# A two-block transformer step on one core: the weight-tile splits near a norm, taken from GpSimd and given to VectorE

## The chip, the core and the metric

The kernel runs on one core of one Trainium2 chip. The metric is device time in microseconds (us) of one execution; lower is better. A core has engines that run side by side, each with its own queue of instructions that it works through in order: TensorE (PE in the profile, its weight loads PEld), VectorE (DVE), ScalarE (ACT), GpSimd (POOL), and SyncE (SP), which here only issues the DMA transfers that bring tiles from device memory.

## The reference

256 tokens of width 1024 go through two blocks, all in float32:

```
first_block:  h = rmsnorm(x); z = h @ w_in
              pool branch, dilated attention, gates;  x = x + merged @ w_out; x = rmsnorm(x) * final_gain
second_block: x += short_conv(rmsnorm(x))
              x += peer(rmsnorm(x))         # 256 tokens against 16384 experts
              x += windowed_gqa(rmsnorm(x))
              x += peer(rmsnorm(x))
              return rmsnorm(x)
peer(xn):     q = xn @ w_q; two top-16 lists of 128 sub-keys per head and token, best 16 pairs g, idx
              out = sum over the 16 of  g * gelu(xn . u[idx]) * v[idx]
```

`peer` is done as two dense products over all 16384 rows of `u` and of `v`, with the chosen weights scattered between them.

## The kernel before

**Splits.** Products are made at float32 accuracy from three matmuls on a faster 32-bit type (`fp32r`): an operand is cut into `hi`, its rounding to that type, and `lo = operand - hi`. Then `a @ b` is `ah@bh + ah@bl + al@bh` (lines 136 to 138). Each weight tile of 128x1024 arrives by DMA as `raw` (four buffers, so that a transfer waits until an older tile has been split), is rounded by ScalarE (`hi`, line 122) and subtracted by `split_now` (`lo`, line 123). Line 123 is given to VectorE or to GpSimd: to GpSimd on every `pool_share`-th tile where a caller asks for that, and also for the first `RELIEF` = 3 streamed tiles behind each norm (`last_rows` sets the counter `relief`).

**Norms.** Between two stages x is updated, normed and transposed. `last_rows` writes this order out by hand: the last products of a stage for token half 1, meanwhile the norm of half 0, then the norm of half 1. The norm of a half is a chain. VectorE adds the two accumulator halves to x (line 234), multiplies by the gain (`xn`, line 303), sums up the mean square (`m`, line 246; into the conv stage `n`, lines 377 and 379), and makes the inverse root in nine tiny steps, lines 256 to 263. It then scales `xn` (line 319, the other half on ScalarE, line 320). TensorE transposes `xn` (line 391), ScalarE and VectorE split the result (`xh`, `xl`, lines 328 and 329), and only then can the next stage multiply. While this goes on for half 1, TensorE has only `first(0)`: the products of half 0 with the first 512 columns of the next stage's weights, held in four tiles `enh`/`enl` that `Enter.split` makes (lines 297 and 298). Of these four, the third (`c == 2`) has its `enl` made by GpSimd, and the other three by VectorE.

**What sets the order.** Outside the hand-written stretches, a list scheduler orders each engine's instructions by priorities. Splits are made ahead of their place (`AHEAD`), norm steps have the highest priority (`CHAIN`), and the result is one fixed queue for each engine. An engine never passes over an instruction that waits.

**The stages**, in us of the profile: first block to 294, conv mixer to 397, first peer to 1208, attention to 1310, second peer to 2115. In the conv mixer the last of eight tiles `o7` is made by VectorE from `pr` (lines 746, 750, 752, 756) and split (lines 402, 403) before the stage's last products; in the first block the last two tiles `mt6`, `mt7` play that part (lines 561, 563, 402, 403).

**Peer queries.** A peer stage begins with sixteen query tiles; n = 4 to 15 go through `dense_t` with `pool_share` 2, so that every second one has its `lo` made by GpSimd.

Of the kernel before, what the change touches and what calls it, by code (L numbers as in the profile page):

```python
# [32 lines left out]
AHEAD, KEEP, CHAIN = 200, 100, 4000  # L33
HL = 3
WARM = 14
RELIEF = 3


JOBS, TURN, J1, J2, LATE, XA = 35, 4, 40, 124, 6, 100
# [11 lines left out]
def two_blocks(ctx: ExitStack, tc: tile.TileContext, io, out):  # L51
    nc = tc.nc
    V, S, G, PE, SY = nc.vector, nc.scalar, nc.gpsimd, nc.tensor, nc.sync
# [18 lines left out]
    def bank(which, name):  # L72
        return which.tile([P, 512], F32, tag="b", name=name)
# [14 lines left out]
           allow_small_or_imprecise_dtypes=True)  # L88


    count, relief, fetched, pin, pinned = [0], [0], [0], [None], [0]
    last_split = [None]

    more = []
# [1 line left out]
    def fetch(src):  # L96

        fetched[0] += 1
        if more and fetched[0] % 3 == 1:
            raw = more[-1].tile([P, D], F32, tag="more", name="more")  # L100
        else:
            raw = stream.tile([P, D], F32, tag="raw", name="raw", bufs=4)
        SY.dma_start(out=raw, in_=src)
        return raw

    def split(raw, pool_share=0, into=None):
        with tc.high_priority(offset=AHEAD):
            return split_now(raw, pool_share, into)

    def split_now(raw, pool_share, into):  # L110
        count[0] += 1
        hi, lo = into or [stream.tile([P, D], F32R, tag=t, name=t, bufs=HL) for t in ("hi", "lo")]
        on_pool = pool_share and count[0] % pool_share == 0
        if relief[0] > 0 and into is None:
            relief[0] -= 1
            on_pool = True
        if pinned[0] > 0 and into is None:
            pinned[0] -= 1
            with tc.issue_after(pin[0]):
                S.copy(out=hi, in_=raw)  # L120
        else:
            S.copy(out=hi, in_=raw)  # L122
        low = (G if on_pool else V).tensor_tensor(out=lo, in0=raw, in1=hi.bitcast(F32),  # L123
                                                  op=OP.subtract)
        if not on_pool:
            last_split[0] = low.ins
        return hi, lo
# [5 lines left out]
    def products(ps, pairs, first, last):  # L133
        n = len(pairs)
        for i, ((ah, al), (bh, bl)) in enumerate(pairs):
            PE.matmul(out=ps, lhsT=ah, rhs=bh, start=first and i == 0, stop=False)  # L136
            PE.matmul(out=ps, lhsT=ah, rhs=bl, start=False, stop=False)  # L137
            PE.matmul(out=ps, lhsT=al, rhs=bh, start=False, stop=last and i == n - 1)  # L138

    def dense_t(src, acts, pool_share=0):  # L140

        ah, al = acts
        hi, lo = split(fetch(src), pool_share)
        ps = bank(p_mm, "mm")[:, :T]
        products(ps, [((hi[:, k * P:(k + 1) * P], lo[:, k * P:(k + 1) * P]), (ah[:, k], al[:, k]))
                      for k in range(8)], True, True)
        return ps
# [48 lines left out]
    def last_rows(nxt, acc0, acc1, steps, scale=None):  # L196


        n = len(steps)
        with tc.manual_schedule(engines={EN.PE, EN.DVE, EN.Activation}):  # L200
            if acc0:
                for half in range(2):
                    add_half(0, half, acc0[half], scale)
                for half in range(2):
                    nxt.added(0, half)
                r = nxt.inverse(0)
                nxt.scaled(0, r)
            for j, step in enumerate(steps):
                if acc0 and j == nxt.turn_at:
                    nxt.turn(0)  # L210
                step()
                if j == n // 2 - 1:
                    add_half(1, 0, acc1[0], scale)
                if j == max(n // 2 - 1, acc0 and nxt.turn_at or 0):
                    nxt.added(1, 0)
            add_half(1, 1, acc1[1], scale)
            nxt.added(1, 1)
            r = nxt.inverse(1)
            nxt.scaled(1, r)
            nxt.first(0)  # L220
            nxt.turn(1)
            nxt.first(1)
            for a in range(2):
                nxt.after(a)
        relief[0] = RELIEF

    def add_half(a, half, acc, scale=None):
        with tc.high_priority(offset=CHAIN):
            s = slice(half * 512, (half + 1) * 512)
            if scale:  # L230
                V.scalar_tensor_tensor(out=x[:, a, s], in0=acc, scalar=scale, in1=x[:, a, s],  # L231
                                       op0=OP.mult, op1=OP.add)
            else:
                V.tensor_tensor(out=x[:, a, s], in0=acc, in1=x[:, a, s], op=OP.add)
            sum_squares(a, half)
# [38 lines left out]
    class Enter:  # L274
# [16 lines left out]
        def split(self, c, d0=0, d1=D, engine=None):  # L291
            if d0 == 0:
                self.kept.append([self.new([P, D], F32R, f"en{w}{c}") for w in "hl"])
            hi, lo = [t[:, d0:d1] for t in self.kept[c]]
            with tc.high_priority(offset=KEEP):
                raw = self.raw[c] if self.raw else fetch(self.columns[c])
                S.copy(out=hi, in_=raw[:, d0:d1])  # L297
                (engine or (G if c == 2 else V)).tensor_tensor(  # L298
                    out=lo, in0=raw[:, d0:d1], in1=hi.bitcast(F32), op=OP.subtract)

        def added(self, a, half, engine=None):
# [462 lines left out]
    def gqa_mixer(entered, nxt):  # L764
        acts, nat = (xh, xl), entered.nat
        with ExitStack() as es:
# [111 lines left out]
            for step in range(18):  # L878
# [42 lines left out]
                if step >= 14:  # L921
                    nxt.split(step - 14)
                    for half in range(2):
                        row(acc1[half], step - 14, 1, half)
            last_rows(nxt, None, acc1, [lambda half=half, n=n: row(acc1[half], n, 1, half)
                                        for half in range(2) for n in range(4, 8)])

    def peer(l, entered, nxt):
        acts, nat = (xh, xl), entered.nat
        with ExitStack() as es:  # L930
            with ExitStack() as es1:
# [19 lines left out]
                def query(n):  # L951
                    if n < 4:
                        q[n] = first[:, n]
                        return
                    ps = dense_t(io["peer_w_q"][l, n - 4], acts, 2)
                    q[n] = X[1][:, n].rearrange("p g t -> p (g t)")
                    S.copy(out=q[n], in_=ps)

# [23 lines left out]
                for n in range(5):  # L982
                    query(n)
# [176 lines left out]
                for i in range(P):  # L1160
# [3 lines left out]
                    for job in at.get(i, []):  # L1164
# [6 lines left out]
                    ps = dense_t(io["peer_u"][l, i], acts, int(i < len(by_pool) and by_pool[i])).rearrange(  # L1171
                        "p (g t) -> p g t", t=4)
# [39 lines left out]
            for i in range(P):  # L1212
# [9 lines left out]
                for a in range(2 if i < P - LATE else 1):  # L1222
                    row(i, a, (0, 1), act, wt)
            last_rows(nxt, acc[0], acc[1], [lambda half=half, n=n, w=w: row(P - LATE + n, 1, [half], *w)
                                            for half in range(2) for n, w in enumerate(late)],
                      1 / G_SCALE)
# [153 lines left out]
```

## Time and profile before

| | |
|---|---|
| median of 3 runs | 2125.38 us (2123.36 to 2125.76) |
| the profiled execution | 2124.93 us, of which 2123.2 us are the span of the profile |
| TensorE busy | 2088.4 us (98%) |
| VectorE busy | 1507.1 us (71%) |
| ScalarE busy | 1092.9 us (51%) |
| GpSimd busy | 218.0 us (10%), 119 instructions |
| DMA | 373.94 MB, mean 176 GB/s |

Busy is the share of the span in which an engine had an instruction under way, and an instruction that has started but is held up counts as busy too. A row of the timeline gives the start, the duration, the engine, the line, the operation, out<-in and the shape; xN means that N alike in a row were put together, and the bracket gives the idle time of the engine before it and what ended it.

### The profile page before, as it was taken

What the parts mean: (1) busy time and instruction counts of PE and PEld (TensorE: products, weight loads), DVE (VectorE), ACT (ScalarE), POOL (GpSimd) and SP (SyncE); (2) the same over time, 40 slices, a digit from 0 to 9 for tenths busy, and PEclk for the clock granted to TensorE, in tenths of its full rate; (3) what the DMA queues carried; (4) which work ended last, traced back from release to release, by engine and by line L of the source; (5) the groups of instructions that cost most, each with busy time, mean ns of one, the idle gap of its engine ahead of it and who ended that gap; (6) DMA issues with size and microseconds to landing.
All of it is one profiled execution on the core that took longest, in us unless ns stands there. A gap on an engine that the chain in (4) does not pass through costs nothing. (4 is left out here: it accounts for less than half of the span.)

```text
span 2123.2 us, 37690 instructions
## 1 busy us (share of the span) xinstructions
PE 2088.4 (98%) x14288; PEld 1897.6 (89%) x14288; DVE 1507.1 (71%) x3101; ACT 1092.9 (51%) x1971; POOL 218.0 (10%) x119
## 2 busy tenths in 40 slices
PE   8999999999999999999999999999999999999998
PEld 7899989899999999888888877999999998888886
DVE  4456778699778887665667485998778885565565
ACT  4556645345555444555556474455554445555553
POOL 3220010263000000000000142540000000000000
PEclk9999999999999999999999999999999999999999
DMA  6645737256655555666667461566555556666663
GB/s 232 221 129 159 236 121 237 91 170 179 183 165 159 161 164 165 191 194 189 192 194 264 146 225 37 173 181 187 160 160 161 167 160 198 191 193 191 190 206 120
DMA packets 104437, 373.94 MB, mean 176 GB/s; under 512 B 12096, under 2 KB 14144, under 8 KB 103744
## 3 DMA queue, kind: packets, MB, share of 16 engines
q1 hardware_dynamic: 103968, 371.01, 56.3%
q8 instruction: 112, 1.84, 0.3%
q14 instruction: 69, 0.57, 0.1%
q10 hardware_dynamic: 288, 0.52, 0.1%
HBM read 370.44 MB, written 1.05 MB: 175 GB/s over the span
## 5 line engine op out<-in xcount | busy, mean ns | idle before, releaser
L136 PE MATMUL mm<-xh,hi 128*128 128x256 f32 x2880 | 830.2, 288 | 0.4 <-DVE k_l L636 0.4
L123 DVE TENSOR_TENSOR lo<-raw,hi 128x1024 fp32r<-128x1024 f32 x532 | 651.9, 1225 | 248.9 <-ACT hi L122 245.6
L137 PE MATMUL mm<-xl,hi 128*128 128x256 f32 x2880 | 813.8, 283 | 0.0
L138 PE MATMUL mm<-xh,lo 128*128 128x256 f32 x2880 | 813.7, 283 | 0.0
L122 ACT CAST hi<-raw 128x1024 fp32r<-128x1024 f32 x600 | 630.0, 1050 | 338.8 <-PE mm L137 188.4
L136 PEld LDWEIGHTS mm<-xh,hi 128*128 128x128 f32 x2880 | 550.8, 191 | 2.6 <-issue 1.3
L137 PEld LDWEIGHTS mm<-xl,hi 128*128 128x128 f32 x2880 | 551.2, 191 | 0.3
L138 PEld LDWEIGHTS mm<-xh,lo 128*128 128x128 f32 x2880 | 550.7, 191 | 0.0
L1204 PE MATMUL acc<-hi,al 128*128 128x512 f32 x976 | 304.4, 393 | 0.5 <-DVE al L1194 0.5
L1204 PE MATMUL acc<-lo,ah 128*128 128x512 f32 x976 | 302.4, 391 | 0.0
L1204 PE MATMUL acc<-hi,ah 128*128 128x512 f32 x976 | 301.8, 390 | 0.2 <-ACT ah L1193 0.2
L1204 PEld LDWEIGHTS acc<-hi,ah 128*128 128x128 f32 x976 | 182.9, 188 | 42.6 <-ACT ah L1193 1.0
L1204 PEld LDWEIGHTS acc<-hi,al 128*128 128x128 f32 x976 | 183.1, 188 | 41.2 <-DVE al L1194 1.8
L1204 PEld LDWEIGHTS acc<-lo,ah 128*128 128x128 f32 x976 | 183.3, 188 | 38.8
L1193 ACT CAST ah<-xa 128x256 fp32r<-128x256 f32 x200 | 81.2, 407 | 241.5 <-PE acc L1204 241.5
L123 POOL TENSOR_TENSOR lo<-raw,hi 128x1024 fp32r<-128x1024 f32 x70 | 173.0, 2473 | 305.8 <-ACT hi L122 291.4
L1194 DVE TENSOR_TENSOR al<-xa,ah 128x256 fp32r<-128x256 f32 x200 | 85.0, 426 | 99.0 <-PE acc L1204 99.0
L1109 DVE TENSOR_TENSOR o<-iota_k,ij 128x1024 f16<-128x1024 f16 x128 | 88.2, 689 | 48.5 <-PE G L1123 48.2
L1133 ACT COPY xa<-G 128x240 f32<-128x240 f32 (+22 forms) x92 | 24.1, 262 | 148.2 <-DVE xa L1130 148.2
L1116 DVE TENSOR_TENSOR wi<-o,gt 128x512 f16<-128x512 f16 x256 | 96.5, 418 | 1.2
L298 POOL TENSOR_TENSOR enl<-raw,enh 128x1024 fp32r<-128x1024 f32 x5 | 12.6, 2524 | 813.8 <-ACT enh L297 813.8
L1123 PE MATMUL G<-wi,o 128*128 128x128 f16 x1024 | 79.8, 220 | 0.0
(461 smaller groups left out, 2016.4 us busy)
## 6 DMA issues: line engine op xcount, KB each, us to landing
raw<-in_peer_u_dram SPq DMA_DIRECT2D x256, 512.0 KB, 3.6
raw<-in_peer_v_dram SPq DMA_DIRECT2D x256, 512.0 KB, 3.6
raw<-in_peer_w_q_dram SPq DMA_DIRECT2D x24, 512.0 KB, 3.8
raw<-in_conv_w_in_dram SPq DMA_DIRECT2D x20, 512.0 KB, 4.5
raw<-in_w_rest_dram SPq DMA_DIRECT2D x18, 512.0 KB, 3.7
raw<-in_w_qk_dram SPq DMA_DIRECT2D x16, 512.0 KB, 4.5
more<-in_w_rest_dram SPq DMA_DIRECT2D x10, 512.0 KB, 3.6
raw<-in_w_v_dram SPq DMA_DIRECT2D x8, 512.0 KB, 4.0
```

Of the source, the lines that this page charges most:

```text
L122: S.copy(out=hi, in_=raw)
L123: low = (G if on_pool else V).tensor_tensor(out=lo, in0=raw, in1=hi.bitcast(F32), op=OP.subtract)
L136: PE.matmul(out=ps, lhsT=ah, rhs=bh, start=first and i == 0, stop=False)
L137: PE.matmul(out=ps, lhsT=ah, rhs=bl, start=False, stop=False)
L138: PE.matmul(out=ps, lhsT=al, rhs=bh, start=False, stop=last and i == n - 1)
L1109: V.tensor_tensor(out=o.rearrange("p n (b c) -> p n b c", c=4), in0=iota_k.rearrange("p (b c) -> p b c", c=4).unsqueeze(1).to_broadcast(fo ...
L1116: V.tensor_tensor(out=wi[i].rearrange("p n (b c) -> p n b c", c=4), in0=o[:, 0:4].rearrange("p n (b c) -> p n b c", c=4), in1=gt[i][:, s]. ...
L1123: PE.matmul(out=ps[:, :, t], lhsT=o[:, 4 + t], rhs=wi[i][:, t], start=i == 0, stop=i == 1)
L1133: S.copy(out=dst[:, old:], in_=ps[:, i0 + old:i0 + n])
L1193: S.copy(out=act[0], in_=src)
L1194: V.tensor_tensor(out=act[1], in0=src, in1=act[0].bitcast(F32), op=OP.subtract)
L1204: PE.matmul(out=acc[a][half], lhsT=p[:, s], rhs=r[:, half * 512:(half + 1) * 512], start=i == 0 and w == 0, stop=i == P - 1 and w == 2)
```

## The change

No split near a norm goes to GpSimd any more: not the three streamed tiles behind it, not the third `enl` tile, and of the peer queries only those from n = 8 on may. Eighteen subtractions of 128x1024 go from GpSimd's queue to VectorE's: 13 of line 123 and 5 of line 298. What is computed stays the same.

```diff
-RELIEF = 3
-    count, relief, fetched, pin, pinned = [0], [0], [0], [None], [0]
+    count, fetched, pin, pinned = [0], [0], [None], [0]
...
         on_pool = pool_share and count[0] % pool_share == 0
-        if relief[0] > 0 and into is None:
-            relief[0] -= 1
-            on_pool = True
...
             for a in range(2):
                 nxt.after(a)
-        relief[0] = RELIEF
...
-                (engine or (G if c == 2 else V)).tensor_tensor(
+                (engine or V).tensor_tensor(
                     out=lo, in0=raw[:, d0:d1], in1=hi.bitcast(F32), op=OP.subtract)
...
-                    ps = dense_t(io["peer_w_q"][l, n - 4], acts, 2)
+                    ps = dense_t(io["peer_w_q"][l, n - 4], acts, 2 * (n >= 8))
```

The queue of SyncE keeps its order. The lines of the changed kernel stand three to five lower (123 is 119 there, 298 is 293). Three places in VectorE's queue matter. The first is the merge at the end of the first block, where the last tiles `mt6` and `mt7` are made; before:

```order
L298 TENSOR_TENSOR enl_3083<-raw,enh_3082 128x1024
L563 TENSOR_TENSOR y<-y 128x256
L561 TENSOR_TENSOR y<-pj,gt_2854 128x256
L298 TENSOR_TENSOR enl_3107<-raw,enh_3106 128x1024
L370 TENSOR_TENSOR gain<-gain,closing 128x1024
L403 TENSOR_TENSOR mt6l<-y,mt6h 128x256
L561 TENSOR_TENSOR y<-pj,gt_2887 128x256
L563 TENSOR_TENSOR y<-y 128x256
L403 TENSOR_TENSOR mt7l<-y,mt7h 128x256
```

and now:

```order
L293 TENSOR_TENSOR enl_3095<-raw,enh_3094 128x1024
L293 TENSOR_TENSOR enl_3107<-raw,enh_3106 128x1024
L365 TENSOR_TENSOR gain<-gain,closing 128x1024
L558 TENSOR_TENSOR y<-y 128x256
L556 TENSOR_TENSOR y<-pj,gt_2854 128x256
L556 TENSOR_TENSOR y<-pj,gt_2887 128x256
L398 TENSOR_TENSOR mt6l<-y,mt6h 128x256
L119 TENSOR_TENSOR lo<-raw,hi 128x1024
L558 TENSOR_TENSOR y<-y 128x256
L119 TENSOR_TENSOR lo<-raw,hi 128x1024
L398 TENSOR_TENSOR mt7l<-y,mt7h 128x256
```

Three splits are new here, and the sum `y` of tile 6 now stands behind two `enl` splits and the product `gain`. The second place is the end of the conv mixer, where `o7` is made; before:

```order
L756 TENSOR_TENSOR z<-y,gb 128x256
L403 TENSOR_TENSOR o6l<-z,o6h 128x256
L123 TENSOR_TENSOR lo<-raw,hi 128x1024
L298 TENSOR_TENSOR enl_4241<-raw,enh_4240 128x1024
L750 TENSOR_SCALAR y<-pr,taps 128x256
L752 SCALAR_TENSOR_TENSOR y<-pr,taps,y 128x256 x2
L756 TENSOR_TENSOR z<-y,gb 128x256
L403 TENSOR_TENSOR o7l<-z,o7h 128x256
```

and now:

```order
L293 TENSOR_TENSOR enl_4223<-raw,enh_4222 128x1024
L398 TENSOR_TENSOR o6l<-z,o6h 128x256
L119 TENSOR_TENSOR lo<-raw,hi 128x1024
L741 TENSOR_TENSOR pr<-mm,gc 128x4x4x16
L293 TENSOR_TENSOR enl_4241<-raw,enh_4240 128x1024
L745 TENSOR_SCALAR y<-pr,taps 128x256
L747 SCALAR_TENSOR_TENSOR y<-pr,taps,y 128x256
L119 TENSOR_TENSOR lo<-raw,hi 128x1024
L747 SCALAR_TENSOR_TENSOR y<-pr,taps,y 128x256
L119 TENSOR_TENSOR lo<-raw,hi 128x1024
L751 TENSOR_TENSOR z<-y,gb 128x256
L398 TENSOR_TENSOR o7l<-z,o7h 128x256
```

One `enl` and two streamed splits have come in among the steps that lead to `o7`. The third place is the norm of half 1 in front of the second peer; before:

```order
L234 TENSOR_TENSOR x<-acc,x 128x512
L303 TENSOR_TENSOR xn_14555<-x,gain 128x512
L234 TENSOR_TENSOR x<-acc,x 128x512
L303 TENSOR_TENSOR xn_14556<-x,gain 128x512
L246 SCALAR_TENSOR_TENSOR m<-ss_80 128x1
```

and now:

```order
L229 TENSOR_TENSOR x<-acc,x 128x512
L298 TENSOR_TENSOR xn_14555<-x,gain 128x512
L119 TENSOR_TENSOR lo<-raw,hi 128x1024
L229 TENSOR_TENSOR x<-acc,x 128x512
L119 TENSOR_TENSOR lo<-raw,hi 128x1024 x2
L298 TENSOR_TENSOR xn_14556<-x,gain 128x512
L241 SCALAR_TENSOR_TENSOR m<-ss_80 128x1
```

All three streamed splits now stand inside the norm. In the norms before the conv mixer and before the first peer one such split stands inside in the same way: ahead of the last `xn`, and ahead of `m`. At the start of the kernel `enl` stands between the inverse root and line 319. In the attention stage the scheduler has also put some twenty instructions of VectorE, ScalarE and TensorE in another order.

## Rows read from the trace of the kernel before

**Rows 1.** From the profile's page: busy time by engine.

```profile
PE 2088.4 (98%) x14288; PEld 1897.6 (89%) x14288; DVE 1507.1 (71%) x3101; ACT 1092.9 (51%) x1971; POOL 218.0 (10%) x119
```

**Rows 2.** The list of waits: who waited for whom; us in total, times, longest.

```profile
DVE x L231 <- PE acc L1204: 28.2, 3, 13.0
...
DVE xb L974 <- PE sc L969: 27.6, 4, 11.7
...
PE tr L391 <- DVE xn L319: 9.7, 4, 3.6
```

**Rows 3.** The instructions that write or read `lo`, those of line 123 on VectorE and on GpSimd: duration in ns, least, median and most; first and last start.

```profile
L123 DVE TENSOR_TENSOR lo<-raw,hi x532: 1204/1225/2611, 25.5 to 2092.2; 128x1024 fp32r<-128x1024 f32 x178
L123 POOL TENSOR_TENSOR lo<-raw,hi x70: 2351/2402/4129, 26.3 to 1432.1; 128x1024 fp32r<-128x1024 f32 x70
```

**Rows 4.** From the page, the groups of instructions: a subtraction of 128x256 on VectorE; busy us, then the mean ns of one.

```profile
L1194 DVE TENSOR_TENSOR al<-xa,ah 128x256 fp32r<-128x256 f32 x200 | 85.0, 426 | 99.0 <-PE acc L1204 99.0
```

**Rows 5.** Timeline of the start of the kernel: the norm of half 1, GpSimd, VectorE, and TensorE behind it.

```profile
15.80 2.80 POOL L298 TENSOR_TENSOR enl<-raw,enh 128x1024 fp32r<-128x1024 f32 x1
...
16.32 2.30 DVE L246 SCALAR_TENSOR_TENSOR m<-ss 128x1 f32<-128x1 f32 x1
18.65 0.16 DVE L256 TENSOR_SCALAR r<-m 128x1 uint32<-128x1 uint32 x1
...
19.99 0.16 DVE L263 SCALAR_TENSOR_TENSOR r<-rt,r 128x1 f32<-128x1 f32 x1
...
20.80 0.47 PE L391 MATMUL tr<-ident,xn 128*128 128x128 f32 x1 [3.62 <-DVE xn L319]
```

**Rows 6.** Timeline of the merge at the end of the first block: VectorE, GpSimd, ScalarE, and TensorE's first use of `mt7l`.

```profile
270.77 2.28 DVE L403 TENSOR_TENSOR mt7l<-y,mt7h 128x256 fp32r<-128x256 f32 x1 [0.47 <-ACT mt7h L402]
274.50 1.39 DVE L234 TENSOR_TENSOR x<-acc,x 128x512 f32<-128x512 f32 x2 [1.44 <-PE acc L181]
...
270.37 4.95 POOL L123 TENSOR_TENSOR lo<-raw,hi 128x1024 fp32r<-128x1024 f32 x2 [5.30 <-DVE y L563]
...
269.24 1.05 ACT L122 CAST hi<-raw 128x1024 fp32r<-128x1024 f32 x1 [2.31 <-DMA raw<-in_conv_w_in_dram]
...
274.06 0.40 PE L181 MATMUL acc<-hi,mt7l 128*128 128x512 f32 x1
```

**Rows 7.** Timeline of the norm of half 1 before the conv mixer: VectorE, GpSimd, TensorE.

```profile
288.38 2.90 DVE L303 TENSOR_TENSOR xn<-x,gain 128x512 f32<-128x512 f32 x1
...
288.17 2.56 POOL L123 TENSOR_TENSOR lo<-raw,hi 128x1024 fp32r<-128x1024 f32 x1 [12.86 <-ACT hi L122]
...
294.88 1.97 PE L391 MATMUL tr<-ident,xn 128*128 128x128 f32 x8 [2.30 <-DVE xn L319]
```

**Rows 8.** Timeline of the end of the conv mixer, where `o7` is made: VectorE, GpSimd, ScalarE, TensorE.

```profile
364.75 2.03 DVE L403 TENSOR_TENSOR o6l<-z,o6h 128x256 fp32r<-128x256 f32 x1 [0.47 <-ACT o6h L402]
...
369.42 2.48 DVE L750 TENSOR_SCALAR y<-pr,taps 128x256 f32<-128x256 f32 x1
371.93 2.96 DVE L752 SCALAR_TENSOR_TENSOR y<-pr,taps,y 128x256 f32<-128x256 f32 x2
...
363.89 2.61 POOL L298 TENSOR_TENSOR enl<-raw,enh 128x1024 fp32r<-128x1024 f32 x1 [73.16 <-ACT enh L297]
369.30 2.44 POOL L123 TENSOR_TENSOR lo<-raw,hi 128x1024 fp32r<-128x1024 f32 x1 [2.80 <-ACT hi L122]
372.07 2.54 POOL L123 TENSOR_TENSOR lo<-raw,hi 128x1024 fp32r<-128x1024 f32 x1 [0.33 <-ACT hi L122]
...
370.89 1.05 ACT L122 CAST hi<-raw 128x1024 fp32r<-128x1024 f32 x1 [1.72 <-DMA raw<-in_peer_w_q_dram]
...
376.00 0.50 PE L181 MATMUL acc<-hi,o7h 128*128 128x512 f32 x1 [4.57 <-ACT o7h L402]
```

**Rows 9.** Timeline of the norm of half 1 before the first peer: VectorE, GpSimd, TensorE.

```profile
392.84 1.99 DVE L246 SCALAR_TENSOR_TENSOR m<-ss 128x1 f32<-128x1 f32 x1 [0.28 <-ACT squares L240]
...
392.32 2.50 POOL L123 TENSOR_TENSOR lo<-raw,hi 128x1024 fp32r<-128x1024 f32 x1 [17.71 <-ACT hi L122]
...
396.95 1.09 PE L391 MATMUL tr<-ident,xn 128*128 128x128 f32 x8 [0.25 <-DVE xn L319]
```

**Rows 10.** Timeline of the norm of half 1 before the second peer: VectorE, GpSimd, ScalarE, TensorE.

```profile
1301.86 1.97 DVE L303 TENSOR_TENSOR xn<-x,gain 128x512 f32<-128x512 f32 x1
1303.75 2.35 DVE L246 SCALAR_TENSOR_TENSOR m<-ss 128x1 f32<-128x1 f32 x1
...
1306.34 2.08 DVE L261 SCALAR_TENSOR_TENSOR rt<-r,m 128x1 f32<-128x1 f32 x1
...
1300.87 7.54 POOL L123 TENSOR_TENSOR lo<-raw,hi 128x1024 fp32r<-128x1024 f32 x3 [18.56 <-ACT hi L122]
...
1299.75 2.93 ACT L122 CAST hi<-raw 128x1024 fp32r<-128x1024 f32 x3
...
1310.18 1.06 PE L391 MATMUL tr<-ident,xn 128*128 128x128 f32 x8 [3.49 <-DVE xn L319]
```

**Rows 11.** Busy time by stretch: start:end, its length, busy us (and instructions) of each engine, the granted share of TensorE's clock, DMA share, GB/s.

```profile
294.70:298.10 3.40, 3.21 (x13) 2.92 (x14) 1.41 (x3) 2.00 (x4) 0.00 (x0) 0.50 0.43 147
...
397.00:400.00 3.00, 2.98 (x18) 2.46 (x19) 1.29 (x2) 2.26 (x5) 0.00 (x0) 1.00 0.28 112
...
1311.90:1315.20 3.30, 3.30 (x11) 2.51 (x10) 0.85 (x2) 0.61 (x2) 0.00 (x0) 0.50 0.00 0
```

## The prediction, made before the changed kernel ran

> **What bounds the kernel now.** I read the busy times first: TensorE has an instruction under way for 98% of the span, no other engine for more than 71% [rows 1], except the weight loads that go with the matmuls. So an edit counts only where TensorE stands still, or where it makes it stand still. In the list of waits TensorE's largest entry is a norm: four waits for the scaled `xn`, 9.7 us together [rows 2]. Another long one, 4.57 us, is for `o7h`, just ahead of a norm [rows 8]. So I read the timeline of VectorE and GpSimd ahead of each of these five, looking for rows that last longer than their like. They are easy to find. `m` adds two columns of 128x1; it takes 2.30 us in one norm, 1.99 and 2.35 in others [rows 5, 9, 10], while the equally small steps behind it take 0.16 [rows 5]. `xn` takes 2.90 us [rows 7] where an add of the same size takes 0.69 (two in 1.39 [rows 6]). Such a row ends with a GpSimd split: `m` at 18.62 and the split at 18.60 [rows 5]; 394.83 and 394.82 [rows 9]. So VectorE is held for as long as GpSimd runs its split, and the splits given to GpSimd stop VectorE in the middle of the chain for which TensorE waits.
>
> Not every row is held. `x<-acc,x`, which reads an accumulator and one tile, takes its usual 0.69 us from 274.50 on, though a GpSimd split runs to 275.32 [rows 6]. The Trainium skill has a rule for this ("SBUF — State Buffer", section "Who interferes with whom"): a VectorE instruction with two inputs in SBUF and a GpSimd instruction that reads SBUF exclude each other, and whichever starts second waits for the other's end. By that rule the trace agrees, in the held rows and in the unheld one, whose accumulator is not in SBUF; the sum below goes by the rows alone.
>
> **The change, part by part.** It moves 18 splits. One takes 2.40 us on GpSimd and 1.22 on VectorE by the medians [rows 3]. Where VectorE was held for a whole one, it now works 1.22 us instead of waiting up to 2.4; where it wasn't held, 1.22 us are new. What counts is how much earlier TensorE starts behind each place.
>
> *Start.* `m` begins at 16.32 and would end after about 0.16, like its neighbours, instead of 18.62. The eight steps from 18.65 to 20.15 take 1.50 us [rows 5]. The split now stands between them and the scaling: 16.32 + 0.16 + 1.50 + 1.22 = 19.2 instead of 20.15. Gain 1.0 us (20.80 for TensorE becomes 19.8).
>
> *Norm before the conv mixer.* An `xn` of 2.90 becomes a split of 1.22 and an `xn` of 0.69 [rows 3, 6, 7]; 2.90 - 1.91 = 1.0 us.
>
> *The tile `o7`.* Line 750, held to 2.48 us until the first streamed split ends at 371.74, and line 752, two in 2.96 until the second ends at 374.61, lead straight to TensorE's start at 376.00, 1.1 us behind line 752's end [rows 8]. `o6l`, held to 2.03, comes ahead of them. Now three splits of 1.22 stand among these steps. The last needs its `hi`, cast from 370.89 to 371.94 as its transfer landed [rows 8]. If that landing doesn't move, the split ends at 373.2 and TensorE starts at 374.3: gain 1.7 us. But the transfer waits for a buffer that GpSimd gave back at 366.50 with the end of its `enl` split; VectorE, idle for 0.47 us before 364.75 [rows 8], makes that split from 364.3 to 365.5, and the landing can come 1.0 us earlier. With that the gain is at most 2.7. I take 2.2, the middle, since the transfer also follows others.
>
> *Norm before the first peer.* `m` is held to 1.99, and one split of 1.22 comes in ahead of it. TensorE stood still for only 0.25 us there, and its first transpose took a little longer [rows 9]; I put 0.4 as the whole gain.
>
> *Norm before the second peer.* Three rows are held: `xn` 1.97, `m` 2.35 and a small step 2.08 [rows 10]. Instead VectorE does three splits. Their casts end one by one until 1302.68, the first at about 1300.8 [rows 10]; from there three splits and the add of 0.69 between them end at 1300.8 + 3 x 1.22 + 0.69 = 1305.1. With `xn` 0.69, `m` 0.16, the eight steps 1.50 and the 0.65 from there to TensorE [rows 5] the transposes start at 1308.1 instead of 1310.18. Gain 2.1 us.
>
> *The merge* is where the change costs something. The `y` of tile 6 comes behind one more `enl` split, two streamed splits stand around the `y` of tile 7, and the cast of the first, from 269.24 to 270.29, now comes ahead of `mt6h`. From there on: `mt6h`, `mt6l`, `y` and `mt7l` at some 0.42 each (as an instruction of the same size does [rows 4]) and two splits of 1.22 end at 270.29 + 1.7 + 2.4 = 274.4. TensorE takes `mt7l` at 274.06 [rows 6]. I put 0.3 us; the bounds are nothing (`mt7l`, held to 2.28 before, ended at 273.05) and 1.3, where TensorE comes 1.0 earlier from the start and the transfers don't.
>
> *At no cost:* the last `enl` tile and the streamed splits where VectorE waits for TensorE: up to 13.0 us before the first add of a norm behind a peer, and up to 11.7 before the first peer list [rows 2]. The query and `enl` splits there are hidden by it; without that cover 1.22 us each. In the attention stage one `enl` split comes in and the hold on its neighbour goes, but the scheduler has also put other instructions in another order; I take 0, and one split either way, 1.2, as the bounds.
>
> *The clock.* Behind the waits for the conv mixer and the second peer TensorE ran at 1.2 GHz, half its clock, for some 3.3 us; behind the 0.25 us at the first peer it stayed at 2.4 (granted 1.00) [rows 11]. Behind `o7h` and at the start it did the same as in those two. Half the clock for 3.3 us costs 1.7. Idle for 2.30 us [rows 7] brought such a spell. By the gains above, 1.3 us (conv mixer) and 1.4 (second peer) are left, between the two cases, and 2.4 (`o7`), beside the upper one. I take one of these three spells as gone, 1.7; the bounds are none and all three, 5.1.
>
> *The sum:* 1.0 + 1.0 + 2.2 + 0.4 + 2.1 - 0.3 + 1.7 = 8.1 us. The profiled execution took 2124.9 us (2123.2 of span), so 2116.8; the median of the runs is 0.5 higher, so 2117.3.
>
> **Rivals.** All times are from the median of 2125.4; 0.2% (4.2 us) is about what a measurement of this kernel can tell from no change.
>
> 1. *The gain is handed on to transfers and casts.* A split whose cast is late now holds all that is queued behind it on VectorE, where GpSimd alone used to wait. For it: the casts at 269.24 and 370.89 both began as a transfer landed [rows 6, 8], and both splits now stand ahead of a step of the chain. Against it: the buffers come free earlier too. It decides at `o7` if that landing comes 1.7 us later than before; then the gain there is nothing. With the merge at -1.3, the attention at -1.2 and no spell gone: 1.0 + 1.0 + 0.4 + 2.1 - 2.5 = 2.0 us, 2123.4. Chance 0.15.
>
> 2. *VectorE becomes the bound in the chains (slower).* If the held rows are long for another reason, GpSimd's splits were free, and each that enters a chain adds 1.22: one at the start, one before the conv mixer, two for `o7`, one before the first peer, three before the second: 8 x 1.22 = 9.8 us, 2135.2. It decides once less than half of the held time goes away. Against it: ends that agree within 0.02 us in two norms, and three holds in one norm while three splits ran. Chance 0.05. The Trainium skill ("Perfetto Trace Analysis", section "Optimizing Scalar/DVE Operations") says that handing work to GpSimd may make sense when VectorE is saturated, with a reservation about the port that both share; at 71% busy, held time included, this VectorE is not saturated, so no run here shows that case.
>
> 3. *All three spells at half clock go.* With the attention at its best: 1.0 + 1.0 + 2.2 + 0.4 + 2.1 - 0.3 + 5.1 + 1.2 = 12.7 us, 2112.7. Chance 0.15.
>
> **How the numbers follow.** The forecast (a gain of 4.2 to 11) has 0.65, the rivals 0.15, 0.05 and 0.15. Forecast and rival 3 lie beyond 0.2%, together 0.80; rival 1 is within; rival 2 is slower. The range from 2112 to 2122.5 holds the bounds of the clock and of `o7`; it leaves out rival 2 and most of rival 1.
>
> **What would show it.** In the profile after, `m` takes 0.15 to 0.2 us in each norm, and `xn` 0.7; TensorE's waits for `xn` of line 319 fall from 9.7 us to about 5.5, the one for `o7h` from 4.57 to about 2.4; the merge has no new wait above 0.5; one spell at 1.2 GHz is gone. The prediction is wrong if VectorE's small steps stay long with GpSimd idle, if splits in the chain wait for their casts, or if TensorE gets a new wait in the merge or in the attention stage.

## The result, and the profile after

The changed kernel takes 2113.32 us (median of 6 runs, 2110.46 to 2116.30); the kernel before took 2124.37 us beside it (6 runs, 2121.70 to 2127.43). The ratio is 0.9949, with a 95% interval from 0.9939 to 0.9959: 11.0 us faster, where 8.1 were forecast. The profiled execution took 2114.89 us, its span is 2113.1 us, 10.1 less than before. The page's busy times, then the list of waits of TensorE:

```profile
PE 2085.9 (99%) x14288; PEld 1895.6 (90%) x14288; DVE 1504.5 (71%) x3119; ACT 1093.2 (52%) x1971; POOL 172.3 (8%) x101
```

```profile
PE tr L386 <- DVE xn L314: 4.8, 3, 2.4
...
PE acc L854 <- ACT zh L844: 0.7, 1, 0.7
PE pv L837 <- ACT p_t L411: 0.7, 1, 0.7
```

VectorE has 18 instructions more and is busy for 2.6 us less than before [rows 1]: what it was held for was counted as its work. The waits for the scaled `xn` fell from 9.7 [rows 2] to 4.8 us, the one for `o7h` from 4.57 [rows 8] to 1.1. Two waits of 0.7 us are new; they are in the attention stage. A third new one, 0.4 us for `lo`, comes up under the third part below. Now the places. The start:

```profile
15.95 0.15 DVE L241 SCALAR_TENSOR_TENSOR m<-ss 128x1 f32<-128x1 f32 x1
...
19.23 1.97 PE L386 MATMUL tr<-ident,xn 128*128 128x128 f32 x8 [2.41 <-DVE xn L314]
```

The norm before the conv mixer (VectorE, TensorE):

```profile
287.40 0.69 DVE L298 TENSOR_TENSOR xn<-x,gain 128x512 f32<-128x512 f32 x1
288.00 0.15 DVE L241 SCALAR_TENSOR_TENSOR m<-ss 128x1 f32<-128x1 f32 x1
...
291.74 1.09 PE L386 MATMUL tr<-ident,xn 128*128 128x128 f32 x8 [1.26 <-DVE xn L314]
```

The end of the conv mixer, where `o7` is made (VectorE, ScalarE, TensorE):

```profile
363.05 0.34 DVE L745 TENSOR_SCALAR y<-pr,taps 128x256 f32<-128x256 f32 x1
...
364.58 1.05 ACT L118 CAST hi<-raw 128x1024 fp32r<-128x1024 f32 x1 [1.41 <-DMA raw<-in_peer_w_q_dram]
...
367.87 0.50 PE L177 MATMUL acc<-hi,o7h 128*128 128x512 f32 x1 [1.13 <-ACT o7h L397]
```

The norm before the second peer:

```profile
1297.58 0.68 DVE L298 TENSOR_TENSOR xn<-x,gain 128x512 f32<-128x512 f32 x1
1298.18 0.15 DVE L241 SCALAR_TENSOR_TENSOR m<-ss 128x1 f32<-128x1 f32 x1
...
1300.54 1.06 PE L386 MATMUL tr<-ident,xn 128*128 128x128 f32 x8 [1.11 <-DVE xn L314]
```

`m` takes 0.15 in each norm where it took 1.99 to 2.35 [rows 5, 9, 10], `xn` 0.68 or 0.69 where it took 2.90 [rows 7] and 1.97 [rows 10], and line 745 takes 0.34 in place of 2.48 [rows 8]. The other held rows are short as well: `rt` 0.22 for 2.08 [rows 10], `o6l` 0.42 for 2.03 [rows 8], the two of line 747 0.49 and 0.48 for 2.96 together [rows 8], `mt7l` 0.42 for 2.28 [rows 6]. Last, the stretches behind the waits (columns as in [rows 11]: the number behind the five engines is the granted clock), first one of before, behind `o7h`, then three of the changed kernel:

```profile
376.60:380.00 3.40, 3.40 (x10) 2.66 (x10) 2.20 (x4) 1.44 (x4) 0.00 (x0) 0.50 0.28 113
```

```profile
291.70:295.10 3.40, 3.34 (x20) 2.74 (x21) 1.98 (x8) 2.35 (x5) 0.00 (x0) 1.00 0.65 225
367.80:371.20 3.40, 3.33 (x15) 2.68 (x16) 2.75 (x5) 1.46 (x5) 0.00 (x0) 1.00 0.71 249
...
1300.40:1303.80 3.40, 3.24 (x19) 2.69 (x20) 1.29 (x2) 2.36 (x5) 0.00 (x0) 1.00 0.29 117
```

TensorE runs at 2.4 GHz (granted 1.00) behind all three waits where it ran at 1.2 GHz before (first row and [rows 11]): three spells are gone, not one. A fourth stays: behind the start's wait of 2.41 us the granted clock is still 0.50.

### The profile page after: what moved, and what is told of

Its sections match the earlier page's. It is cut to its first block, busy times and chain, and to the rows that moved or that the text cites. A ratio compares the mean times of both kernels' runs of the same rounds, so it can differ in the third digit from the quotient of the medians.

```text
span 2113.1 us, 37679 instructions
## 1 busy us (share of the span) xinstructions
PE 2085.9 (99%) x14288; PEld 1895.6 (90%) x14288; DVE 1504.5 (71%) x3119; ACT 1093.2 (52%) x1971; POOL 172.3 (8%) x101
## 5 line engine op out<-in xcount | busy, mean ns | idle before, releaser
L119 DVE TENSOR_TENSOR lo<-raw,hi 128x1024 fp32r<-128x1024 f32 x545 | 666.1, 1222 | 271.3 <-ACT hi L118 268.0
L119 POOL TENSOR_TENSOR lo<-raw,hi 128x1024 fp32r<-128x1024 f32 x57 | 139.2, 2442 | 1151.6 <-DMA raw<-in_attn_w_q_dram 663.9
L1125 DVE TENSOR_TENSOR xa<-G,xa 128x400 f32<-128x400 f32 (+31 forms) x128 | 60.8, 475 | 11.0 <-PE G L1118 10.7
```

The lines of the kernel that those rows point to most:

```text
L1125: V.tensor_tensor(out=dst[:, :old], in0=ps[:, i0:i0 + old], in1=dst[:, :old], op=OP.mult)
```

## The experiments

**The parts alone.** First the streamed splits and the queries without the `enl` tiles. Against the changed kernel:

```diff
-                (engine or V).tensor_tensor(
+                (engine or (G if c == 2 else V)).tensor_tensor(
```

> The change without its second part: the streamed splits and the peer queries go to VectorE as in the changed kernel, the third enl tile of each of the five entries stays on GpSimd as before. Theory (a GpSimd split holds VectorE, each place has its own price): the gain of the start (1.5 us of waiting and its share of the half-clock spell, 2.0 together) is lost, the 2.1 us that the changed kernel lost in the attention stage come back, since its instructions stand in the order of before, and at o7 some 1 us is lost, since the enl split holds o6l and gives a buffer back late: 2113.3 + 2.0 - 2.1 + 1.0 = 2114.2 us, from 2113 to 2115.5. The waits of TensorE for o7h and for the scaled xn before the conv mixer and the second peer stay at 1.1 to 2.1 us. Rival (the gains hang on the two parts together, each alone still leaves a hold in each chain): 2118 or more.

Measured: 2114.97 us, ratio 0.9953 (0.9940 to 0.9966). Nearly the whole gain is in the streamed splits and queries. At `o7` the GpSimd split holds `o6l` (2.44 us), TensorE waits 2.15 us for `o7h`, and a spell at 1.2 GHz is there again:

```profile
371.54 0.79 PE L177 MATMUL acc<-hi,o7h 128*128 128x512 f32 x1 [2.15 <-ACT o7h L397]
```

```profile
371.50:374.70 3.20, 3.16 (x8) 2.48 (x9) 1.31 (x3) 0.72 (x2) 0.00 (x0) 0.50 0.68 224
```

Then the `enl` tiles alone, against the kernel before:

```diff
-                (engine or (G if c == 2 else V)).tensor_tensor(
+                (engine or V).tensor_tensor(
```

> The other part alone: only the third enl tile goes to VectorE, the three streamed splits behind each norm and the peer queries stay as before. Theory: the start gains 2.0 us, o7 up to 1.0, the attention stage loses 2.1; the holds in the norms before the conv mixer and the second peer stay (m or xn of about 2 us or more), and with them the spells at 1.2 GHz behind them. 2124.4 - 2.0 - 0.5 + 2.1 = 2123.9 us, from 2122.5 to 2125.5, about the same as before. Rival (the parts act together): 2119 or less.

Measured: 2126.71 us, ratio 1.0010 (1.0001 to 1.0019), 1.2 us above the range expected. The profiled execution, 2124.94 us, lies inside that range, so its trace can't show the whole miss. It shows two losses that were not expected: a wait of 1.17 us for `pr` at 348.25, whose cause is not shown, and one in the merge (VectorE, GpSimd, TensorE):

```profile
269.18 2.43 DVE L403 TENSOR_TENSOR mt6l<-y,mt6h 128x256 fp32r<-128x256 f32 x1 [1.07 <-ACT mt6h L402]
271.53 2.60 DVE L563 TENSOR_TENSOR y<-y 128x256 f32<-128x256 f32 x1
...
268.92 4.92 POOL L123 TENSOR_TENSOR lo<-raw,hi 128x1024 fp32r<-128x1024 f32 x2 [132.69 <-ACT hi L122]
...
274.62 0.50 PE L181 MATMUL acc<-hi,mt7h 128*128 128x512 f32 x1 [1.13 <-ACT mt7h L402]
```

With VectorE's steps in the new order the two streamed splits, still on GpSimd, fall on `mt6l` and on the sum `y` of tile 7, and TensorE waits 1.13 us for `mt7h`, which it does neither before nor in the full change. So the parts do not add up: one moved a hold to a worse place, the other takes it away. The start gave less than the 2.0 us expected: the transposes begin at 19.71, 1.1 us earlier than before.

The third part undone:

```diff
-                    ps = dense_t(io["peer_w_q"][l, n - 4], acts, 2 * (n >= 8))
+                    ps = dense_t(io["peer_w_q"][l, n - 4], acts, 2)
```

> The changed kernel without its third part: peer queries from n = 4 on may again go to GpSimd, so that two of the four tiles n = 4 to 7 of each peer do (n = 5 and n = 7). The first of them stands in the chain of o7 or of the norm before the second peer, beside steps with two inputs in SBUF. Theory (each GpSimd split in a chain holds one step there by up to 2.4 us, in place of 1.22 of work): the last scaled add of o7 and the last xn or m before the second peer are held again, by about 1.2 us net each, and one spell at 1.2 GHz (1.3 to 1.5 us) comes back: 2113.3 + 2.4 + 1.4 = 2117 us, from 2114.5 to 2118.5. Rival (this part moves only splits that lie hidden behind other work): 2113 to 2114.

Measured: 2115.24 us, ratio 0.9957 (0.9945 to 0.9969); no difference from the full change can be told. The theory was right that holds come back, and wrong on their price. At `o7` it is `o7l` that is held (1.99 us) and not the last add, and before the second peer it is `xn`:

```profile
368.82 0.50 PE L177 MATMUL acc<-hi,o7l 128*128 128x512 f32 x1 [1.29 <-DVE o7l L398]
...
1293.75 2.18 DVE L298 TENSOR_TENSOR xn<-x,gain 128x512 f32<-128x512 f32 x1
```

TensorE waits 1.29 us for `o7l` and nothing for `o7h`, where the full change waits 1.13 us for `o7h`; before the second peer it waits 1.59 instead of 1.11 us. That is about 0.2 and 0.5 us, not 1.2 each, and no spell came back behind either (granted 1.00). So the third part is worth less than the times can tell.

The full change's new wait of 0.40 us for `lo` is not its doing. It follows a hold that the change left: GpSimd's split of a tile of `u` and the VectorE step `ra` start 0.16 us apart in the full change (first three rows) and 0.14 with the third part undone (last two). In one the step is held, in the other the split:

```profile
507.21 2.50 POOL L119 TENSOR_TENSOR lo<-raw,hi 128x1024 fp32r<-128x1024 f32 x1 [0.79 <-ACT hi L118]
507.37 2.49 DVE L1039 TENSOR_TENSOR ra<-ra,m__6108 128x128 f32<-128x128 f32 x1
...
518.57 0.39 PE L134 MATMUL mm<-xh,lo 128*128 128x256 f32 x1 [0.40 <-DVE lo L119]
```

```profile
507.72 4.09 POOL L119 TENSOR_TENSOR lo<-raw,hi 128x1024 fp32r<-128x1024 f32 x1 [0.81 <-ACT hi L118]
...
507.86 0.28 DVE L1039 TENSOR_TENSOR ra<-ra,m__6108 128x128 f32<-128x128 f32 x1
```

The kernel with the `enl` tiles alone, whose queries are those of before, has the same pair in its second peer: `ra` takes 2.49 us from 1431.32, and TensorE waits 0.39 us at 1442.53. What decides which of the two is held is not shown.

**The attention stage.** One split of the 18 given back, the third `enl` tile of the last entry (`thirds` counts the entries):

```diff
-                (engine or V).tensor_tensor(
+                (engine or (G if c == 2 and (thirds.append(c) or len(thirds) == 5) else V)).tensor_tensor(
```

> The changed kernel with one split of the 18 given back to GpSimd: the third enl tile of the last entry, into the second peer, which is made in the attention stage. With it TensorE's order in the attention stage is that of before. Theory (the 2.1 us that were lost there come from the order, in which TensorE waits 0.68 us each for p_t and for zh): the two waits are gone, the offset between the kernels stays at 9.3 us through the stage, and the time is 2111.2 us, from 2110.5 to 2112. Rival 1 (the loss comes from VectorE's added work there, or is chance): the time stays within 0.5 us of the changed kernel's 2113.3. Rival 2 (the split holds VectorE there and costs as much): 2113.5 or more.

Measured: 2111.19 us, ratio 0.9938 (0.9925 to 0.9951). The intervals overlap with the full change's, so the trace has to decide. The first row is TensorE's wait for `s`, early in the stage, of before, the second the same of the full change; its end is in [rows 10] and above. Third and fourth are both ends of this kernel:

```profile
1239.65 0.30 PE L413 MATMUL tr<-ident,s 128*128 128x128 f32 x1 [3.07 <-DVE s L827]
```

```profile
1230.09 0.30 PE L408 MATMUL tr<-ident,s 128*128 128x128 f32 x1 [3.05 <-DVE s L822]
```

```profile
1231.49 0.45 PE L408 MATMUL tr<-ident,s 128*128 128x128 f32 x1 [3.06 <-DVE s L822]
...
1299.27 1.07 PE L386 MATMUL tr<-ident,xn 128*128 128x128 f32 x8 [1.09 <-DVE xn L314]
```

From there to the transposes, without the wait for `xn`: 70.53 - 3.49 = 67.0 us before, 70.45 - 1.11 = 69.3 in the full change, 67.78 - 1.09 = 66.7 here. So taking that one split from GpSimd had cost 2.3 us, and the waits for `p_t` and `zh` are not in this kernel's list. The kernel with the `enl` tiles alone, where the five are on VectorE too, has both waits again (0.7 us each). That the order which the scheduler makes of it did this, and not VectorE's 1.22 us, is argued: the two were not parted.

**Is it the reading?** Two kernels have all the change's splits on VectorE and an idle instruction on GpSimd at each streamed tile behind a norm; one reads and one (but for one column) only writes. `near` counts three tiles behind each norm, `spare` is a tile of 832 bytes per partition:

```diff
+        if near[0] > 0 and into is None:
+            near[0] -= 1
+            G.tensor_tensor(out=spare, in0=raw[:, :832], in1=hi[:, :832].bitcast(F32), op=OP.subtract, saturate=False)
```

```diff
+        if near[0] > 0 and into is None:
+            near[0] -= 1
+            G.tensor_copy(out=spare[:, 0:2].bitcast(F32), in_=hi[:, 0:1].bitcast(F32))
+            for _ in range(6):
+                G.memset(spare, 0.0)
```

> The changed kernel, every split where the change puts it, plus one idle instruction on GpSimd for each of the three streamed tiles behind a norm: it subtracts 832 of the 1024 columns of the same two tiles into a spare tile that nobody reads (about 1.95 us each by the 2.40 of a whole split). VectorE's work and TensorE's work are those of the changed kernel. Theory (a GpSimd instruction that reads its operands in SBUF holds a VectorE step with two inputs there): the steps in the chains (m, xn, the steps of o7, mt6l and y in the merge) are held again by up to 2 us on top of VectorE's own splits: before the conv mixer +1.9, o7 +3, the first peer +1, the second peer +3, the merge +1.6, and three spells at 1.2 GHz of 1.4: 2113.3 + 14.7 = 2128 us, from 2120 to 2133, no faster than before. Rival (VectorE was slow for another reason, the split's place in its queue or a wait for the cast): 2113 to 2114.5.

> The same places, but GpSimd only writes there: a copy of one column of hi (so that it starts as late as a split would), then six times a memset of the spare tile, 128x416, some 2.7 us together. Theory (only GpSimd's reads hold VectorE's second input): m stays at 0.15 us and xn at 0.69 in every norm, and the time is that of the changed kernel, 2113.3 us within 1. Rival (any work of GpSimd holds VectorE): as in the kernel where it reads, 2120 or more, with m or xn of 2 us or more.

Measured: 2126.39 us where it reads (ratio 1.0016, 1.0006 to 1.0025), 2104.68 us where it writes (0.9920, 0.9902 to 0.9938). The second was 8 us faster than the changed kernel, which no theory had. So a control was needed, the spare tile alone with one memset at the start:

```diff
+    spare = const.tile([P, 416], BF16, name="spare")
+    G.memset(spare, 0.0)
```

> The control for the two kernels with a spare tile: the changed kernel with the spare tile of 832 bytes per partition in the same place and one memset of it at the start, no work of GpSimd behind the norms. The two kernels with the spare tile both had matmuls of another pace than all the others: 117 instead of 120 ns from one 128x256 matmul of a dense product to the next, 233 instead of 229 ns for the 128x512 matmuls with the rows of v. The tile moves the addresses of all tiles allocated behind it. Theory (the address alone does it, and GpSimd's writes cost nothing): 117 and 233 ns again and 2104.7 us, from 2103 to 2107. Rival (the writes of GpSimd brought it): 120 and 229 ns and 2113 us.

Measured: 2105.61 us (0.9913, 0.9896 to 0.9929). So the 8 us are the tile's (see the last section), and against this control GpSimd's writes cost nothing that can be told (0.9 us less) and its reads 20.8 us. (The profiled executions of control and reads lie 27.3 us apart. Of these, some 5.5 us come from no wait: early in both peers the products with `xh` ran slower where GpSimd reads, 513 matmuls in 60 us against 531; see the last section. Most of the rest lies at the waits and the spells behind them. The kernel that reads also gives `raw` back later, which the one that writes does not; whether later transfers have a share in it was not tested.) The 2128 us that I had expected came out nearly right by two errors: the base was 8 us lower, and the reads cost 6 us more than I had put. The norm before the second peer, first with the reads, then with the writes:

```profile
1304.01 5.34 DVE L120 TENSOR_TENSOR lo<-raw,hi 128x1024 fp32r<-128x1024 f32 x2
1309.27 2.42 DVE L303 TENSOR_TENSOR xn<-x,gain 128x512 f32<-128x512 f32 x1
...
1302.31 8.83 POOL L124 TENSOR_TENSOR spare<-raw,hi 128x832 fp8e4<-128x832 f32 x3 [22.05 <-ACT hi L119]
...
1313.96 1.30 PE L391 MATMUL tr<-ident,xn 128*128 128x128 f32 x5 [5.82 <-DVE xn L319]
```

```profile
1283.76 1.23 DVE L120 TENSOR_TENSOR lo<-raw,hi 128x1024 fp32r<-128x1024 f32 x1 [1.06 <-ACT hi L119]
...
1285.51 2.35 DVE L120 TENSOR_TENSOR lo<-raw,hi 128x1024 fp32r<-128x1024 f32 x2
1287.78 0.68 DVE L305 TENSOR_TENSOR xn<-x,gain 128x512 f32<-128x512 f32 x1
...
1283.79 1.25 POOL L124 COPY spare<-hi 128x1 f32<-128x1 f32 x1 [22.04 <-ACT hi L119]
1285.10 2.96 POOL L126 MEMSET spare<- 128x416 bf16 x6
```

The two splits took 5.34 instead of 2.35 us and `xn` 2.42 instead of 0.68, and the holding goes both ways: GpSimd's copy of a single column lasted 1.25 us, to 1285.04, while VectorE's split ran to 1284.99. The Trainium skill has the same ("SBUF — State Buffer", section "Who interferes with whom": two inputs in SBUF contend with a GpSimd instruction that reads SBUF, not with one that only writes it); by that rule, these rows agree.

**The clock.** In the kernel before, idle matmuls fill the waits before the conv mixer and the second peer (`norms` counts the calls):

```diff
             nxt.first(0)
+            norms[0] += 1
+            if norms[0] in (1, 4):
+                ps = bank(p_tr, "warm")
+                for _ in range(6 if norms[0] == 1 else 10):
+                    PE.matmul(out=ps[:, 0:P], lhsT=ident, rhs=ident, start=True, stop=True)
             nxt.turn(1)
```

> The kernel before, with idle matmuls of 128x128 put into TensorE's queue where it waits for the scaled xn: six before the conv mixer (wait 2.30 us) and ten before the second peer (3.49 us). They fill the greater part of the wait and do nothing else. Theory (the spell at 1.2 GHz behind a wait comes from TensorE having stood still, and costs 1.3 to 1.5 us): both spells are gone, the transposes start no later than before, and the time falls by 2.7 us, from 2124.4 to 2121.7, from 2120.5 to 2123. Rival (the spell has another cause, such as the transposes themselves): granted clock 0.50 behind both waits as before, and 2124 to 2125.

Measured: 2121.98 us, ratio 0.9988 (0.9979 to 0.9998). Behind both filled waits the granted clock is 1.00 (0.50 in [rows 11]):

```profile
294.00:297.40 3.40, 2.44 (x18) 1.87 (x17) 1.93 (x6) 2.27 (x4) 0.00 (x0) 1.00 0.60 163
1308.00:1312.00 4.00, 3.55 (x21) 2.90 (x22) 1.66 (x3) 2.74 (x5) 0.00 (x0) 1.00 0.33 114
```

So the spells come from standing still. The two cost some 2 us by the medians, less than the 3.4 of my price of 1.7. By the traces, from the first transpose to the same product behind the spell, they cost 1.2 (4.05 to 2.86 us) and 1.5 (5.75 to 4.26).

**What is chance in the profile of before.** The same kernel once more.

> The kernel before, profiled once more, to see what of its profile is chance. In the profile shown, the transfer of the last kept weight tile ahead of o7 took 6.2 us from issue to landing, where its like take 4.2 to 4.9. If that is chance: it takes under 5 us this time, o7h is waited for some 3 us instead of 4.57, and 1.5 us of what the changed kernel gained at o7 were never the change's. If it belongs to the kernel: 6 us again, and the wait for o7h is 4 us or more.

Measured: 2121.56 us in its one run. The transfer took 4.45 us this time, so the 6.2 were chance, but the wait for `o7h` is still 4.01 (ScalarE, TensorE):

```profile
367.02 1.05 ACT L122 CAST hi<-raw 128x1024 fp32r<-128x1024 f32 x1 [1.29 <-DMA raw<-in_peer_w_q_dram]
...
372.99 0.79 PE L181 MATMUL acc<-hi,o7h 128*128 128x512 f32 x1 [4.01 <-ACT o7h L402]
```

So by this one profile 0.6 us of the 3.4 gained there were chance, not the 1.5 expected. The last cast, from 367.02, comes 2.0 us ahead of TensorE's wait (it began at 368.98); in the profile shown it came only 0.5 ahead, in the changed kernel 2.2.

**All splits to VectorE:** `on_pool = False` in the changed kernel.

> The changed kernel with no split left on GpSimd at all: another 63 go to VectorE, which was busy for 1504.5 us of 2113. Theory (a GpSimd split is never free for VectorE, and VectorE has room): in the attention stage the scaling of s (2.59 us for two instructions that take 0.62 elsewhere) and a step on two columns (1.52) are no longer held, the wait of 3.1 us for s there becomes shorter by 1 to 2 us; the queries and the first block hide their new splits behind TensorE: 2111 us, from 2108.5 to 2113. Rival (VectorE becomes the bound in the attention stage, where it was busy for 15.65 of 18.00 us): a wait for a split there, 2114 us or more.

Measured: 2113.62 us, ratio 0.9949 (0.9932 to 0.9967), the same as the changed kernel. Both theories hold in part: the waits for `s` fell from 4.9 to 1.4 us and the transposes before the second peer start 4.1 us earlier (1296.40), but of that lead the span keeps 2.1 (2111.0): the rest is lost in the second peer, between 1410 and 1438 us, where TensorE waits for a split again (0.48 us at 1428.95). Giving VectorE the other splits too wins nothing.

## Why the prediction came out as it did

| step | predicted, us | measured, from TensorE's rows |
|---|---|---|
| start | 1.0 | 1.6 (20.80 to 19.23), of which 0.4 stood before `m` began; 1.1 (19.71) in the kernel with the fifth split back, whose start is the same |
| norm before the conv mixer | 1.0 | 1.0 (wait 2.30 to 1.26) |
| `o7` | 2.2 (1.7 to 2.7) | 3.4 (4.57 to 1.13), or 2.9 against before profiled again |
| norm before the first peer | 0.4 | the wait of 0.25 is gone |
| norm before the second peer | 2.1 | 2.4 (3.49 to 1.11) |
| merge | -0.3 | 0: `mt7l` is used 2.1 us earlier (271.95 for 274.06), about the lead from the start |
| attention | 0 (-1.2 to 1.2) | -2.3 |
| spells at 1.2 GHz | one gone, 1.7 | three gone: 1.2, 1.55 and 1.5 |

The mechanism was right at each place where a hold was named. (The eight tiny steps of the sums are nine; their 1.50 us are right.) The sum of the measured waits without the clock is 1.6 + 1.0 + 3.4 + 0.25 + 2.4 - 2.3 = 6.35 us, where 6.4 were forecast (8.1 - 1.7): two errors, `o7` too small and attention too good, cancel by luck. The three spells, each from TensorE's start behind the wait to the same product in both kernels, were worth 4.05 - 2.85, 3.96 - 2.41 and 5.75 - 4.22, together 4.3 us. That makes 10.6; the span lost 10.1, and the 0.5 between are small steps both ways, such as the new wait for `lo`.

*The clock* is the term that was mis-sized. I expected 1.3, 1.4 and 2.4 us of standing still to be left and let one spell in three go; 1.26, 1.11 and 1.13 were left, and none brought a spell, nor did 1.59 with the third part undone, while 2.15 in the kernel with the streamed part alone did. A spell cost 1.2 to 1.55 us, not 1.7. On the clock the third rival was right, with a chance of 0.15; that its time (2112.7) is so near the measured one is luck, since it had the attention at +1.2 where -2.3 came.

*The tile `o7`* is why the third wait came out low: its gain passed my upper bound of 2.7, by 0.2 even against the second profile of before. The sum took the last cast from the one profile shown, where it was late by chance. From the cast of the second profile the same sum gives 368.07 + 1.22 + 1.11 = 370.4 instead of 372.99, a gain of 2.6 where 2.9 were measured.

*The attention stage* failed as a step. I had seen that twenty instructions stood in another order and gave it the price of one split; TensorE's new waits for `p_t` and `zh` (0.7 us each) came with that order, and the 2.3 us lie beyond my bounds. *At no cost* held as far as the traces show: the one new wait for a split, 0.40 us, follows a hold that the change left in place, and a kernel without the moved queries has it too.

The first rival did not come about: the landing at `o7` came earlier (its cast began at 364.58 instead of 370.89 [rows 8], 6.3 us, where TensorE's lead ahead of its wait was 8.1 - 3.4 = 4.7). The second was refuted by the changed kernel's own `m`, and by the kernel where GpSimd reads: the same VectorE work as its control, 20.8 us apart, with splits and `xn` held again.

## What to carry to other kernels

When a tiny VectorE instruction lasts microseconds, look which GpSimd instruction ends with it: handing work to GpSimd beside a serial chain can cost more than doing it. Profile the kernel before twice, and work the sum from both: one late transfer moved a bound here. Price a shorter wait with the clock behind it, and treat a reordered queue as a cost of its own, to be read row by row. Test the parts of a change together and apart, and give any kernel with an added tile a control that has the tile alone.

## What the hardware showed that was not expected

In these kernels the address of a tile changes TensorE's pace. The spare tile moves all tiles allocated behind it by 832 bytes, and that alone was worth 8 us. Two more kernels have the fifth `enl` split on GpSimd and two pads of 320 bytes; one pad stands ahead of the peer's tiles (`ah`, `al`), the other ahead of `xh` in the first kernel and behind `xl` in the second:

```diff
+    pad = const.tile([P, 80], F32, name="pad")
+    G.memset(pad, 0.0)
...
+                pad2 = kept.tile([P, 80], F32, name="pad2")
+                G.memset(pad2, 0.0)
```

> The changed kernel with the fifth third tile back on GpSimd (2111.2 us) and two pads of 320 bytes, one ahead of xh, one ahead of the peer's tiles, so that xh, xl, hi, lo, ah and al all begin at a multiple of 512 bytes. In the kernel before, xh and hi begin 192 bytes past such a multiple and ah 384; with the spare tile, hi began at one, xh and ah 192 past it. Theory A (what counts is where the weights of a matmul begin, 512 best, 64 worst): 117 ns or less for the products with xh, 226 ns or less for those with ah, 8640 x 2.7 = 23 us and 2928 x 3 = 9 us less: 2079 us, from 2072 to 2090. Theory B (what counts is how the two operands of a matmul lie to each other, and equal is slow): 120 and about 226 to 233 ns, 2104 to 2122 us.

> The changed kernel with the fifth third tile back on GpSimd, and with the two pads of 320 bytes placed otherwise: one behind xh and xl, one ahead of the peer's tiles. So hi, lo, ah and al begin at a multiple of 512 bytes, and xh and xl 192 past one, as before. The runs so far, by the bytes past a multiple of 512: products with xh take 120 ns with xh and hi both at 192, 120 with both at 0, 117 with xh at 192 and hi at 0; products with ah take 229 with hi at 192 and ah at 384, 233 with 0 and 192, 227 with 0 and 0. If it is these remainders that count: 117 and 227 ns, and from the fifth_back kernel's 2111.2 us 8640 x 2.7 = 23 and 2928 x 2.2 = 6 less, 2082 us, from 2078 to 2090. If it is another property of the address (a larger multiple, or what lies between the tiles): 120 ns stay with xh, 2105 us.

Measured: 2105.33 us (0.9914, 0.9897 to 0.9930) and 2088.34 us (0.9832, 0.9814 to 0.9851). The count of TensorE's matmuls (first bracket) in 100 us of the products with `xh` and in 100 us of those with `ah`, for the changed kernel, the spare tile alone, the first pads and the second:

```profile
600.00:700.00 100.00, 100.00 (x924) 99.01 (x924) 80.98 (x156) 51.04 (x139) 0.00 (x0) 1.00 0.53 163
900.00:1000.00 100.00, 100.00 (x438) 82.05 (x437) 59.97 (x74) 53.13 (x73) 0.00 (x0) 1.00 0.64 192
```

```profile
600.00:700.00 100.00, 100.00 (x940) 98.94 (x938) 82.30 (x158) 50.89 (x142) 0.00 (x0) 1.00 0.53 164
900.00:1000.00 100.00, 100.00 (x431) 80.98 (x430) 59.16 (x72) 51.91 (x71) 0.00 (x0) 1.00 0.60 188
```

```profile
600.00:700.00 100.00, 100.00 (x924) 99.01 (x924) 80.98 (x156) 51.13 (x139) 0.00 (x0) 1.00 0.53 163
900.00:1000.00 100.00, 100.00 (x443) 82.81 (x442) 60.94 (x74) 53.40 (x75) 0.00 (x0) 1.00 0.63 194
```

```profile
600.00:700.00 100.00, 100.00 (x938) 98.94 (x937) 82.61 (x159) 50.95 (x141) 0.00 (x0) 1.00 0.53 166
900.00:1000.00 100.00, 100.00 (x443) 82.81 (x442) 60.93 (x74) 53.44 (x75) 0.00 (x0) 1.00 0.62 194
```

With `xh` (the operand that streams) and `hi` (the weights) both 192 or both 0 bytes past a multiple of 512, 924 matmuls fit; with 192 and 0, 938 to 940. For `hi` (streaming here) and `ah` (the weights): 438 with 192 and 384, 431 with 0 and 192, 443 with 0 and 0. Theory A (weights best at a multiple of 512) fails on the products with `xh`: 924 with `hi` at 0, as with `hi` at 192. Theory B (equal is slow) fails on those with `ah`: 443 with both at 0. The remainders forecast the last kernel (2082 expected, within its range to 2090), but which property of the address decides stays open. That kernel is the fastest of all here, 1.7% below before.

The remainders can't be all. In the kernel where GpSimd only writes, the products with `xh` early in the first peer and at the same place in the second, with the same `xh` and `xl` and the same three buffers of `hi` and `lo`, run at two paces:

```profile
420.00:480.00 60.00, 60.00 (x532) 60.00 (x531) 57.13 (x239) 29.21 (x43) 31.47 (x13) 1.00 0.62 183
1310.00:1370.00 60.00, 60.00 (x514) 60.00 (x513) 56.62 (x306) 26.56 (x39) 38.15 (x16) 1.00 0.56 174
```

At the same places the control has 531 and 531, the kernel that reads 513 and 514, the changed kernel 506 and 505. So in the kernels with moved tiles these addresses alone do not set the pace. In the second peer that is 3.0 us between the control and this kernel, and what sets it is not shown.
